# Gain rows by a broadcasting DMA instead of GpSimd, and other start addresses for token and weight tiles

## The chip, the cores and the metric

The kernel runs on one core of a Trainium2 chip. Its time is the device time of one execution in microseconds; lower is better. The core has five engines with instruction streams of their own: TensorE (PE in the profile, its weight loads as PEld), VectorE (DVE), ScalarE (ACT), GpSimd (POOL) and SyncE (SP), which here only issues transfers. Engines wait for each other by semaphores.

## What is computed

One decoder layer on 512 tokens of width 1024, float32: a SwiGLU block, a mixer that joins differential attention and an SSD scan, and a second SwiGLU block, each between two RMS norms with a gain row of 1024 values.

```python
def rms_norm(x, g):
    xf = x.astype(jnp.float32)
    y = xf * lax.rsqrt(jnp.mean(xf * xf, axis=-1, keepdims=True) + EPS)
    return (y * g.astype(jnp.float32)).astype(x.dtype)

def swiglu(h, w_gate, w_up, w_down):
    return (jax.nn.silu(h @ w_gate) * (h @ w_up)) @ w_down

def hybrid_layer(x, ...):
    h = rms_norm(x, ffn1_pre_g)
    x = x + 0.5 * rms_norm(swiglu(h, ffn1_w_gate, ffn1_w_up, ffn1_w_down), ffn1_post_g)
    h = rms_norm(x, mix_pre_g)
    proj = h @ w_in
    ...
    attn = diff_attention(q, k, v, lam, attn_subln_g, lambda_init)
    ssm = ssd_mixer(z, xbc, dt, conv_w, conv_b, dt_bias, a_log, d_skip, ssm_norm_g)
    mixed = jnp.concatenate([attn, ssm], axis=-1) @ w_out
    x = x + rms_norm(mixed, mix_post_g)
    h = rms_norm(x, ffn2_pre_g)
    x = x + 0.5 * rms_norm(swiglu(h, ffn2_w_gate, ffn2_w_up, ffn2_w_down), ffn2_post_g)
    return x
```

Seven gain rows are used: ffn1_pre, ffn1_post, mix_pre, mix_post, ffn2_pre (fetched twice, at the end of the mixer and at the start of the second block) and ffn2_post. Tokens lie on the 128 partitions where a norm is applied, so every partition needs the whole row.

## The kernel before

Three stages follow one another, `f1` (first SwiGLU), `mix` and `f2` (second SwiGLU). The 512 tokens are four tiles t = 0 to 3 of 128. A float32 operand is split into a high and a low part, and a product is three TensorE products (high x high, high x low, low x high): L219 to L221 are those of `mm3`, L396 the first lead product in another order, L450 the down projection, L327 the products of gate and up. These last go by a seven-product scheme over halves of the tokens and columns: VectorE and ScalarE make sums of weight halves (L286 to L309) and of token halves (L248 to L270), and 3360 products of 256 columns at L327 use them. Most weights come as 0.5 or 1 MB loads into `raw`, ScalarE casts the high part (L201, L291), VectorE subtracts the low part (L202, L292), and both stand in `w` in the SwiGLU stages and in `whi`/`wlo` in the mixer. `hb` holds the normalised, transposed tokens, `S` their sums, `hid` the hidden values, `ac` the accumulators.

A stage opens by normalising: the square and its sum on ScalarE (`sumsq`, L169), the reciprocal root on GpSimd (`rstd`, L162 a tensor_scalar, L163 a power with the constant `mhalf`), the scaling by root and gain on VectorE (L178), eight transposes per tile on TensorE (L183), the split into `hb` on ScalarE and VectorE (L187). In `f1` tiles 0 and 1 come first and the lead products follow; in `f2` tiles 0 and 1 are done as the mixer ends, and tiles 2 and 3 after the lead products of the first half of the tokens.

The gain of such a norm comes from `bcast` (L150 to L156): SyncE loads the row of 4 KB into one partition of a tile, and GpSimd's partition_broadcast (L155) writes it to all 128 partitions of a second tile. The 49 mixer parameters (`prm`, L140) go the same way. GpSimd also makes the 128x1024 products of the SSD steps (L808, tiles `kb` from `ah` and `al`), which L820 sums on TensorE (`decay`), sums of token halves (L248), masks, and it issues the stores of x. In the SSD steps TensorE goes by turns over attention (L748 transposes, L753 values), the decay products (L814, L820) and, as filler, projection products (L217 to L221); the gains `mix_post_g` and `ffn2_pre_g` are fetched there.

Within each engine the order is a list that a scheduler writes when the kernel is built; an instruction waits for its operands and for its buffer, and what stands behind it on its engine waits too. Tiles are placed one behind the other in the buffer in the order in which their tags first appear.

Of the kernel before, what the change touches and what calls it, by code (L numbers as in the profile page):

```python
# [11 lines left out]
F32 = mybir.dt.float32  # L12
# [5 lines left out]
P = 128  # L18
D = 1024
# [10 lines left out]
class Layer:  # L30
# [14 lines left out]
    @contextmanager  # L45
    def in_stage(s, name):

        with s.tc.tile_pool(name=name, bufs=1, reuse_waits="tile") as pool:
            s.stage, s.ffn_stage = pool, name != "mix"
            yield  # L50

    def blk(s, shape, dt=F32):
# [41 lines left out]
    def consts(s):  # L94
        nc = s.nc
        s.ident = s.t([P, P], F32, "ident")
        make_identity(nc, s.ident)
        s.mhalf = s.t([P, 32], F32, "mhalf")[:, :8]
        nc.gpsimd.memset(s.mhalf, -0.5)

    def mixer_consts(s, conv_w, conv_b, dt_bias, a_log, d_skip, subln, norm_g, lq1, lk1, lq2, lk2):
        nc = s.nc
        s.ones = s.t([P, P], F32, "ones")
        nc.gpsimd.memset(s.ones, 1.0)
        s.u1 = s.t([P, P], F32, "u1")
        nc.gpsimd.affine_select(s.u1, s.ones, pattern=[[-1, P]], base=-1, channel_multiplier=1,
                                compare_op=ALU.is_ge, fill=0.0)
        s.u2 = s.t([P, P], F32, "u2")
        nc.gpsimd.affine_select(s.u2, s.ones, pattern=[[1, P]], base=0, channel_multiplier=-1,
                                compare_op=ALU.is_ge, fill=0.0)  # L110

        rows = s.m((P, P))
        nr = 61 + 8
        nc.sync.dma_start(rows[0:48, :], conv_w.rearrange("k (t p) -> (k t) p", p=P))
        nc.sync.dma_start(rows[48:60, :], conv_b.rearrange("o (t p) -> (o t) p", p=P))
        nc.sync.dma_start(rows[60:61, 0:64], subln)
        nc.sync.dma_start(rows[60:61, 64:128], subln)
        nc.sync.dma_start(rows[61:69, :], norm_g.rearrange("o (t p) -> (o t) p", p=P))
        ps = s.pb()
        nc.tensor.transpose(ps[:, :nr], rows[:nr, :], s.ident[:nr, :nr])  # L120
        s.cols = s.t([P, nr], F32, "cols")
        nc.vector.tensor_scalar_mul(s.cols, ps[:, :nr], 0.5)
        nc.vector.tensor_scalar_mul(s.cols[:, 60:61], ps[:, 60:61], 1.0 - LAMBDA_INIT)

        row = s.m((1, 48 + 128))
        nc.sync.dma_start(row[:, 0:16], dt_bias)
        nc.sync.dma_start(row[:, 16:32], a_log)
        nc.sync.dma_start(row[:, 32:48], d_skip)
        for i, l in enumerate((lq1, lq2, lk1, lk2)):
            nc.sync.dma_start(row[:, 48 + 32 * i:80 + 32 * i], l)  # L130
        lam = s.t([1, 4], F32, "lam")
        nc.vector.tensor_mul(row[:, 48:112], row[:, 48:112], row[:, 112:176])
        nc.vector.tensor_reduce(lam[:, 0:2], row[:, 48:112].rearrange("p (a b) -> p a b", a=2),
                                axis=AX.X, op=ALU.add)
        nc.scalar.activation(lam[:, 0:2], lam[:, 0:2], AF.Exp)
        nc.scalar.activation(row[:, 16:32], row[:, 16:32], AF.Exp)
        nc.vector.tensor_scalar(row[:, 48:49], lam[:, 1:2], lam[:, 0:1], -LAMBDA_INIT,
                                op0=ALU.subtract, op1=ALU.add)
        s.prm = s.t([P, 49], F32, "prm")
        nc.gpsimd.partition_broadcast(s.prm, row[:, 0:49])  # L140
        s.nlam = s.prm[:, 48:49]

        s.qscale = s.t([P, 4], F32, "qscale")
        s.nslope = s.t([P, 48], F32, "nslope")[:, :16]
        for h in range(8):
            lo = (h % 2) * 64
            nc.gpsimd.memset(s.qscale[lo:lo + 64, h // 2:h // 2 + 1], 32.0 ** -0.5 * 2.0 ** (h + 1))
            nc.gpsimd.memset(s.nslope[:, 2 * h:2 * h + 2], -2.0 ** -(h + 1))

    def bcast(s, ap):  # L150
        nc = s.nc
        row = s.k4([1, D])
        nc.sync.dma_start(row, ap)
        t = s.k4([P, D])
        nc.gpsimd.partition_broadcast(t, row)  # L155
        return t  # L156


# [79 lines left out]
    def sums_of_h(s, h):  # L238

        nc, v = s.nc, s.nc.vector  # L240
        tmp = lambda: s.t([P, 4, 256], F32, "hid", 6, s.stage)
        a1 = []
        S1, S2, S3, S4 = (None,) * 4

        def first():
            for b in range(2):
                f = tmp()
                nc.gpsimd.tensor_tensor(f, h[b][0][:, :, :256].bitcast(F32), h[b][1][:, :, :256].bitcast(F32), op=ALU.add)  # L248
                a1.append(f)

        st = {}

        def more(t):
            ts = slice((t - 2) * P, (t - 1) * P)

            def f(p21, p22):
                if t == 2:
                    for n in range(1, 5):
                        st[n] = tmp()
                S1, S2, S3, S4 = (st[n][:, :, ts] for n in range(1, 5))  # L260
                a11, a12 = (a[:, :, ts] for a in a1)
                v.tensor_copy(S3, p21)
                v.tensor_sub(S1, p22, S3)
                v.tensor_sub(S3, a11, S3)
                v.scalar_tensor_tensor(S2, a11, -1.0, S1, op0=ALU.mult, op1=ALU.subtract)
                v.scalar_tensor_tensor(S4, a12, -1.0, S2, op0=ALU.mult, op1=ALU.subtract)
            return f

        def part(hi, lo, x):
            nc.scalar.copy(hi, x)  # L270
            v.tensor_sub(lo, x, hi)
            return hi, lo

        def end():
            A = {n: part(*(s.t([P, 4, 256], F32R, "S", 6, s.stage) for _ in range(2)), st[n]) for n in (3, 2, 4)}

            A[1] = part(*(h[0][i][:, :, 256:] for i in range(2)), st[1])
            return A

        return first, more, end  # L280
# [29 lines left out]

    def gate_up(s, A, wg, wu, i):

# [4 lines left out]
        def product(ps, a, b, first):  # L317
# [3 lines left out]
            for m in range(2):  # L321
                cs = slice(256 * m, 256 * m + 256)
                (ah, al), (wh, wl) = A[a], W[m][b]
                for k in range(4):
# [49 lines left out]
    def ffn(s, h, wg, wu, wd, gain, finish, prepare, fetch=(), late=()):  # L374
# [26 lines left out]
        for half in range(2):  # L401
            for i, (j, w) in enumerate(lead):
# [9 lines left out]
                product(banks[i], lw[i], slice(256 * half, 256 * half + 256), i == 0, ins if half == 0 else None)  # L412
        A = end()
        for b in range(2):
            for half in range(2):
                A.setdefault((11, 12)[b] + 10 * half, tuple(x[:, :, 256 * half:256 * half + 256] for x in h[b]))
        for pi, (i0, i1) in enumerate(parts):
# [721 lines left out]
```

## Time and profile before

| | us |
|---|---|
| median of 3 runs | 1156.06 (1155.16 to 1157.9) |
| the profiled execution | 1153.56 |
| its span | 1151.9 |
| PE busy in it | 1057.1 |
| DVE busy | 785.5 |
| ACT busy | 505.7 |
| POOL busy | 107.6 |

The span is the time from the first to the last record of the profiled execution. TensorE records are pipelined: the duration of one product (0.28 us for 256 columns) reaches beyond the start of the next, so the pace is read from start to start. A row of the timeline tells when an instruction started, how long it took and, in brackets, how long its engine had been idle and which engine ended that; "issue" there means that the profile shows nothing that it waited for. PEclk is the granted TensorE clock, 1.00 the upper of its two levels.

### The profile page before, as it was taken

To read this page: it belongs to the slowest core of one execution; us is meant where nothing else is said; L and a number is where in the kernel's file an instruction comes from. 1 tells how busy PE (TensorE), PEld (TensorE's weight loads), DVE (VectorE), ACT (ScalarE), POOL (GpSimd) and SP (SyncE) were. 2 spreads that over 40 slices of the span, in tenths; PEclk is the share of its full clock that TensorE was granted. 3 is DMA by queue.
4 is the path that set the end of the run, shared out by engine and by line. 5 is a ranking of instruction groups with operands and counts; after the bars stand their busy time and mean duration, and the time that the engine had idled before them with its cause. 6 is when DMAs were issued, how large, how long until landed. Compare 5 with 4: busy or idle time off the path is not lost. (4 is left out here: it accounts for less than half of the span.)

```text
span 1151.9 us, 16496 instructions
## 1 busy us (share of the span) xinstructions
PE 1057.1 (92%) x6569; PEld 943.2 (82%) x6569; DVE 785.5 (68%) x1189; ACT 505.7 (44%) x861; POOL 107.6 (9%) x132
## 2 busy tenths in 40 slices
PE   1999999999999789999996999967999999999997
PEld 1989898998898667888875777857898989988985
DVE  1977686775775733686885987675776867747745
ACT  2555343542453433465652455433653534524532
POOL 1300000000000310000013441031000000000001
PEclk9999999999999889999998999978999999999999
DMA  2523242242223254643321103054232422422232
GB/s 91 201 74 113 71 147 74 79 142 74 83 83 112 77 163 139 162 127 104 92 74 37 46 29 110 1 189 140 74 110 74 147 74 76 144 74 74 86 117 91
DMA packets 94821, 114.44 MB, mean 99 GB/s; under 512 B 5069, under 2 KB 74769, under 8 KB 94744
## 3 DMA queue, kind: packets, MB, share of 16 engines
q1 hardware_dynamic: 93592, 109.20, 30.4%
q0 software_dynamic: 1152, 4.19, 0.9%
q8 instruction: 51, 0.84, 0.3%
q14 instruction: 26, 0.21, 0.1%
HBM read 100.79 MB, written 6.29 MB: 93 GB/s over the span
## 5 line engine op out<-in xcount | busy, mean ns | idle before, releaser
L327 PE MATMUL pa<-hb,w 128*128 128x256 f32 x960 | 128.5, 284 | 5.7 <-DVE at L341 5.0
L327 PE MATMUL pa<-S,w 128*128 128x256 f32 x960 | 126.8, 283 | 4.3 <-ACT cv L357 4.3
L327 PE MATMUL pt<-hb,w 128*128 128x256 f32 x960 | 129.3, 283 | 0.6 <-DVE w L292 0.6
L327 PEld LDWEIGHTS pa<-hb,w 128*128 128x128 f32 x960 | 122.4, 192 | 8.8 <-DVE at L341 5.8
L327 PEld LDWEIGHTS pa<-S,w 128*128 128x128 f32 x960 | 120.7, 192 | 6.1 <-ACT cv L357 5.1
L327 PEld LDWEIGHTS pt<-hb,w 128*128 128x128 f32 x960 | 122.0, 192 | 1.6 <-DVE w L292 0.8
L292 DVE TENSOR_TENSOR w<-raw,w 128x1024 fp32r<-128x1024 f32 x80 | 97.6, 1221 | 30.9 <-PE pa L327 12.7
L202 DVE TENSOR_TENSOR w<-raw,w 128x1024 fp32r<-128x1024 f32 x52 | 72.0, 1395 | 58.2 <-PE pa L327 25.4
L291 ACT CAST w<-raw 128x1024 fp32r<-128x1024 f32 x80 | 83.9, 1049 | 57.9 <-PE pa L327 43.9
L450 PE MATMUL pb<-w,hid 128*128 128x512 f32 x384 | 96.8, 393 | 1.2 <-ACT hid L370 1.1
L201 ACT CAST w<-raw 128x1024 fp32r<-128x1024 f32 x52 | 54.0, 1048 | 95.9 <-PE pa L327 48.2
L450 PEld LDWEIGHTS pb<-w,hid 128*128 128x128 f32 x384 | 70.2, 189 | 14.5 <-ACT hid L370 1.6
L202 DVE TENSOR_TENSOR wlo<-raw,whi 128x1024 fp32r<-128x1024 f32 x44 | 53.3, 1221 | 36.3 <-ACT whi L201 36.0
L327 PE MATMUL pt<-S,w 128*128 128x256 f32 x480 | 64.0, 284 | 3.3 <-ACT S L270 2.5
L298 DVE TENSOR_TENSOR T<-raw 128x1024 f32<-128x1024 f32 x40 | 48.9, 1221 | 24.2 <-DMA raw<-in_ffn_w_up_dram 12.7
L155 POOL PARTITION_BROADCAST w<-w x5 | 6.7, 1342 | 620.1 <-DMA w<-in_ffn_post_g_dram 301.9
L450 PE MATMUL pa<-w,hid 128*128 128x512 f32 x192 | 64.5, 395 | 0.0
L220 PE MATMUL pa<-hb,whi 128*128 128x512 f32 x160 | 64.4, 402 | 0.0
L327 PEld LDWEIGHTS pt<-S,w 128*128 128x128 f32 x480 | 60.3, 191 | 4.7 <-ACT S L270 2.9
L221 PE MATMUL pa<-hb,wlo 128*128 128x512 f32 x160 | 64.1, 401 | 0.0
L201 ACT CAST whi<-raw 128x1024 fp32r<-128x1024 f32 x44 | 45.6, 1049 | 42.0 <-PE pa L220 32.8
L291 ACT CAST w<-T 128x1024 fp32r<-128x1024 f32 x40 | 42.1, 1052 | 44.4 <-PE po L450 22.6
(285 smaller groups left out, 2203.8 us busy)
## 6 DMA issues: line engine op xcount, KB each, us to landing
raw<-in_ffn_w_gate_dram SPq DMA_DIRECT2D x20, 1024.0 KB
raw<-in_ffn_w_up_dram SPq DMA_DIRECT2D x20, 1024.0 KB
raw<-in_ffn_w_down_dram SPq DMA_DIRECT2D x16, 1024.0 KB
raw<-in_w_in_dram SPq DMA_DIRECT2D x32, 512.0 KB
raw<-in_ffn_w_down_dram SPq DMA_DIRECT2D x12, 512.0 KB
blk<-kc SPq DMA_DIRECT2D x96, 64.0 KB
raw<-in_w_out_dram SPq DMA_DIRECT2D x12, 512.0 KB
x_d<-ac POOLq DMA_DIRECT2D x8, 512.0 KB, 4.9
```

The costliest lines, as they stand in the source:

```text
L155: nc.gpsimd.partition_broadcast(t, row)
L201: s.nc.scalar.copy(hi, raw)
L202: s.nc.vector.tensor_sub(lo, raw, hi)
L220: mm(ps, a[0], b[1], start=False, stop=False)
L221: return mm(ps, a[1], b[0], start=False, stop=last).ins
L291: nc.scalar.copy(hi, x)
L292: v.tensor_sub(lo, x, hi)
L298: v.tensor_add(T13.rearrange("p (h k) f -> p h k f", h=2), r[:, 0:4, :].rearrange("p k (h f) -> p h k f", h=2), odd.rearrange("p (h k) f - ...
L327: i = mm(ps[:, cs], x[:, k, :], y[:, k, :], start=first and head is None, stop=k == 3 and x is wl, skip_group_check=True)
L450: nc.tensor.matmul(pd[c], a[:, ts], w[:, c * S:(c + 1) * S], start=st, stop=sp)
```

## The change

1. `bcast` loads the row straight into all 128 partitions: one DMA whose source repeats the 4 KB row 128 times, 512 KB written. GpSimd's broadcast and the one-partition tile are gone.
2. `prm` is made by TensorE, a product of a row of ones with the 49 values into a PSUM bank, and a VectorE copy.
3. `mhalf` grows from 32 to 40 columns, a tile `place` of 64 bytes a partition is allotted at the head of the two SwiGLU stages, and another, `place_S`, ahead of `S`. Nothing is ever written to them: they move the start addresses of all that follows. As built, every large tile of the kernel before starts at a multiple of 128 bytes. After the change `hb`, `S`, `T` and `ac` start 32 bytes past such a multiple, `w`, `hid` and `raw` of the two SwiGLU stages 96 past, and all tiles of the mixer 32 past.

```diff
--- before.py
+++ after.py
@@ -47,6 +47,8 @@
 
         with s.tc.tile_pool(name=name, bufs=1, reuse_waits="tile") as pool:
             s.stage, s.ffn_stage = pool, name != "mix"
+            if s.ffn_stage:
+                s.t([P, 16], F32, "place", 1, pool)
             yield
 
     def blk(s, shape, dt=F32):
@@ -95,7 +97,7 @@
         nc = s.nc
         s.ident = s.t([P, P], F32, "ident")
         make_identity(nc, s.ident)
-        s.mhalf = s.t([P, 32], F32, "mhalf")[:, :8]
+        s.mhalf = s.t([P, 40], F32, "mhalf")[:, :8]
         nc.gpsimd.memset(s.mhalf, -0.5)
 
     def mixer_consts(s, conv_w, conv_b, dt_bias, a_log, d_skip, subln, norm_g, lq1, lk1, lq2, lk2):
@@ -137,7 +139,9 @@
         nc.vector.tensor_scalar(row[:, 48:49], lam[:, 1:2], lam[:, 0:1], -LAMBDA_INIT,
                                 op0=ALU.subtract, op1=ALU.add)
         s.prm = s.t([P, 49], F32, "prm")
-        nc.gpsimd.partition_broadcast(s.prm, row[:, 0:49])
+        ps = s.pb()
+        nc.tensor.matmul(ps[:, 0:49], s.ones[0:1, :], row[:, 0:49], start=True, stop=True)
+        nc.vector.tensor_copy(s.prm, ps[:, 0:49])
         s.nlam = s.prm[:, 48:49]
 
         s.qscale = s.t([P, 4], F32, "qscale")
@@ -149,10 +153,8 @@
 
     def bcast(s, ap):
         nc = s.nc
-        row = s.k4([1, D])
-        nc.sync.dma_start(row, ap)
         t = s.k4([P, D])
-        nc.gpsimd.partition_broadcast(t, row)
+        nc.sync.dma_start(t, ap.broadcast_to([P, D]))
         return t
 
 
@@ -272,6 +274,7 @@
             return hi, lo
 
         def end():
+            s.t([P, 16], F32, "place_S", 1, s.stage)
             A = {n: part(*(s.t([P, 4, 256], F32R, "S", 6, s.stage) for _ in range(2)), st[n]) for n in (3, 2, 4)}
 
             A[1] = part(*(h[0][i][:, :, 256:] for i in range(2)), st[1])
```

Lines from L155 on stand two or three lines further down in the changed kernel (L162 is L164 there, L183 is L185, L219 to L221 are L221 to L223, L327 is L330, L808 is L811, L820 is L823).

The scheduler gives another order at three places. SyncE's list at the start of `f1`, before (w_75 and w_76 are x's tiles 0 and 1, w_80 the gain):

```order
L1062 DMA w_75<-in_x_dram 128x1024
L153 DMA w_80<-in_ffn_pre_g_dram 1x1024
L210 DMA raw_137<-in_ffn_w_gate_dram 128x8x128
L210 DMA raw_168<-in_ffn_w_up_dram 128x8x128
L210 DMA raw_201<-in_ffn_w_gate_dram 128x8x128
L1062 DMA w_76<-in_x_dram 128x1024
L210 DMA raw_232<-in_ffn_w_up_dram 128x8x128
```

and now:

```order
L1065 DMA w_76<-in_x_dram 128x1024
L157 DMA w_81<-in_ffn_pre_g_dram 128x1024
L1065 DMA w_77<-in_x_dram 128x1024
L212 DMA raw_136<-in_ffn_w_gate_dram 128x8x128
L212 DMA raw_167<-in_ffn_w_up_dram 128x8x128
L212 DMA raw_200<-in_ffn_w_gate_dram 128x8x128
L212 DMA raw_231<-in_ffn_w_up_dram 128x8x128
```

The gain has become a full tile, and x's second tile has moved from behind three weight loads to right behind the gain.

GpSimd's list where the SSD steps begin, before; a bare "ISA" at a line is a change of its library, the ISA with ka tiles the broadcast:

```order
L808 TENSOR_TENSOR kb_5630<-u_545_3757,ah_4230 128x1024
L155 ISA
L155 ISA ka_6676<-ka_6674 128x1024
L808 ISA
L808 TENSOR_TENSOR kb_5632<-u_545_3757,al_4231 128x1024
L155 ISA
L155 ISA ka_6680<-ka_6678 128x1024
L808 ISA
L808 TENSOR_TENSOR kb_5648<-u_545_3757,ah_4230 128x1024
L808 TENSOR_TENSOR kb_5650<-u_545_3757,al_4231 128x1024
```

and now:

```order
L811 TENSOR_TENSOR kb_5628<-u_544_3753,ah_4228 128x1024
L811 TENSOR_TENSOR kb_5630<-u_544_3753,al_4229 128x1024
L811 TENSOR_TENSOR kb_5646<-u_544_3753,ah_4228 128x1024
L811 TENSOR_TENSOR kb_5648<-u_544_3753,al_4229 128x1024
L811 TENSOR_TENSOR kb_5764<-u_544_3753,ah_4228 128x1024
```

Six of the ten rows are gone, and the `kb` products of the first steps stand in a row. The same holds at every other broadcast; GpSimd's list has 129 rows where it had 151, and the only bare ISA left is the one at the masks at the very start.

TensorE's list at the start of `f2`, before (pa is the last lead product of the first half but one, po the last, pt and pb the transposes of tiles 2 and 3):

```order
L221 MATMUL pa_7011<-hb_6767,w_7008 128x256
L219 MATMUL po_7042<-hb_6765,w_7038 128x256
L183 MATMUL pt_7055<-ident_63,w_7053 128x128 x4
L183 MATMUL pt_7062<-ident_63,w_7053 128x128 x4
L220 MATMUL po_7042<-hb_6766,w_7038 128x256
L221 MATMUL po_7042<-hb_6765,w_7039 128x256
```

and now:

```order
L221 MATMUL po_7035<-hb_6759,w_7031 128x256
L222 MATMUL po_7035<-hb_6760,w_7031 128x256
L223 MATMUL po_7035<-hb_6759,w_7032 128x256
L221 MATMUL po_7035<-hb_6761,w_7031 128x256
L222 MATMUL po_7035<-hb_6762,w_7031 128x256
L185 MATMUL pt_7048<-ident_63,w_7046 128x128 x4
L185 MATMUL pt_7055<-ident_63,w_7046 128x128 x4
L223 MATMUL po_7035<-hb_6761,w_7032 128x256
L185 MATMUL pb_7079<-ident_63,w_7077 128x128 x4
```

The transposes of tile 2 stood behind the first product of po; they now stand behind its first 14, and those of tile 3 one product later.

## Rows read from the trace of the kernel before

**Rows 1.** The page, part 1: engine, busy us (share), xinstructions.

```profile
PE 1057.1 (92%) x6569; PEld 943.2 (82%) x6569; DVE 785.5 (68%) x1189; ACT 505.7 (44%) x861; POOL 107.6 (9%) x132
```

**Rows 2.** Waits of PE: waiting <- awaited: us in total, times, longest.

```profile
PE pt L183 <- DVE w L178: 30.1, 3, 22.0
PE pb L820 <- POOL kb L808: 12.2, 2, 10.1
```

**Rows 3.** Line 155: ns min/median/max, first to last start us.

```profile
L155 POOLq MODIFY_POOL_CONFIG  x12: 1/11/15, 1.6 to 792.8; - x12
L155 POOL PARTITION_BROADCAST w<-w x5: 1302/1302/1499, 12.1 to 1093.2; - x5
```

**Rows 4.** Timeline of POOL, start: us, duration, instruction, [idle <-releaser].

```profile
12.09 1.30 POOL L155 PARTITION_BROADCAST w<-w  x1 [10.47 <-issue]
20.33 0.18 POOL L162 TENSOR_SCALAR r<-ss 128x1 f32<-128x1 f32 x1 [6.94 <-issue]
```

**Rows 5.** Windows: PE, PEld, DVE, ACT, POOL busy, PEclk, DMA, GB/s.

```profile
4.00:10.00 6.00, 0.00 (x0) 0.00 (x0) 0.00 (x0) 1.15 (x2) 0.00 (x0) 1.00 1.06 335
10.00:20.00 10.00, 0.00 (x0) 0.00 (x0) 0.00 (x0) 0.00 (x0) 1.30 (x1) 1.00 0.01 3
```

**Rows 6.** Timeline of ACT and PE, the start.

```profile
4.53 1.06 ACT L169 ACTIVATE w<-w 128x1024 f32<-128x1024 f32 x1 [2.46 <-DMA w<-in_x_dram]
24.52 1.06 ACT L169 ACTIVATE w<-w 128x1024 f32<-128x1024 f32 x1
29.22 2.08 PE L396 MATMUL pa<-hb,w 128*128 128x256 f32 x8
```

**Rows 7.** Timeline of POOL, the start of the SSD steps.

```profile
590.44 1.84 POOL L155 PARTITION_BROADCAST ka<-ka  x1 [6.39 <-PE pt L748]
600.05 1.89 POOL L808 TENSOR_TENSOR kb<-u,al 128x1024 fp32r<-128x1024 f32 x1 [7.77 <-PE pt L748]
607.87 1.56 POOL L155 PARTITION_BROADCAST ka<-ka  x1 [5.93 <-ACT cv L594]
616.55 1.89 POOL L808 TENSOR_TENSOR kb<-u,ah 128x1024 fp32r<-128x1024 f32 x1 [7.12 <-issue]
```

**Rows 8.** Timeline of PE, the start of the SSD steps.

```profile
618.49 1.22 PE L820 MATMUL pb<-kb,u1r 128*128 128x512 f32 x2 [10.11 <-POOL kb L808]
619.51 0.63 PE L217 MATMUL pa<-hb,whi 128*128 128x512 f32 x1
...
621.64 0.54 PE L221 MATMUL pa<-hb,wlo 128*128 128x512 f32 x1
...
622.48 0.40 PE L217 MATMUL pa<-hb,whi 128*128 128x512 f32 x1
...
625.92 0.39 PE L217 MATMUL pa<-hb,whi 128*128 128x512 f32 x1
```

**Rows 9.** Timeline of POOL and ACT, the start of f2.

```profile
778.61 1.31 POOL L155 PARTITION_BROADCAST w<-w  x1 [5.94 <-issue]
789.68 0.18 POOL L162 TENSOR_SCALAR r<-ss 128x1 f32<-128x1 f32 x1 [9.77 <-issue]
779.55 1.04 ACT L169 ACTIVATE w<-ac 128x1024 f32<-128x1024 f32 x1
```

**Rows 10.** Timeline of PE, the start of f2.

```profile
783.84 0.28 PE L219 MATMUL po<-hb,w 128*128 128x256 f32 x1
792.01 1.94 PE L183 MATMUL pt<-ident,w 128*128 128x128 f32 x8 [7.89 <-DVE w L178]
...
794.18 0.41 PE L219 MATMUL po<-hb,w 128*128 128x256 f32 x1
794.39 0.41 PE L220 MATMUL po<-hb,w 128*128 128x256 f32 x1
```

**Rows 11.** Windows, columns as in Rows 5: products in f2.

```profile
980.00:1000.00 20.00, 20.00 (x167) 19.96 (x166) 14.88 (x22) 12.56 (x22) 0.00 (x0) 1.00 0.40 142
```

**Rows 12.** The page, part 5: a group of line 327.

```profile
L327 PE MATMUL pa<-hb,w 128*128 128x256 f32 x960 | 128.5, 284 | 5.7 <-DVE at L341 5.0
```

## The prediction

> **What bounds the kernel now.** I read the engine totals first. TensorE is busy 1057.1 of the 1151.9 us span, 92%, and VectorE 68% [rows 1]; so the time is TensorE's own work plus the stretches in which it stands still, and the second thing to read is what it stood still for. Two of its waits are larger than any other: the transposes of L183 waited 30.1 us in three pieces, the longest 22.0, for VectorE's scaled rows, and L820 waited 12.2 us in two pieces for a GpSimd product [rows 2]. Both lead to GpSimd, which is busy only 9% [rows 1]. So I read its instructions around those waits, and what it did before each. Line 155, the partition broadcast, costs 1.30 us itself and comes with pool-configuration commands, 12 of them on that line [rows 3]. What is long is the silence around it: 10.47 us before the first broadcast and 6.94 us before the tiny operation that follows it, which belongs to the other library [rows 4]. The same pair stands around every broadcast: 6.39 and 7.77, 5.93 and 7.12 us in the SSD steps [rows 7], 5.94 and 9.77 us at the start of f2 [rows 9]. Five of the eight end by "issue", that is, on nothing the profile shows; the other three have the same length, so I read all eight as the switch of libraries.
>
> There are eight broadcasts, seven of gains and one of parameters. Four of them, two ahead of the first FFN's end, one ahead of the second's and that of the parameters, hold up nothing that TensorE waits for. The other four stand at three places, which I take in order.
>
> **Part 1: the start.** x's first tile is there at 4.53 us, and the square of the second stands at 24.52, queued on ScalarE behind casts that need the first scaled tile; the first product follows at 29.22, 4.70 us after that square [rows 6]. All loads are in at about 10 us: 335 GB/s from 4 to 10, 3 GB/s after [rows 5]. After the change the first scaled tile waits for x, the gain and a reciprocal root, no library. The gain is now 512 KB instead of 4 KB; on SyncE's queue it stands behind x's first tile and the second tile right behind it, ahead of the weights. At 335 GB/s it takes 1.6 us, so the gain is in at about 6.1 and the second tile at 7.7; the square of that tile then runs 4.70 us before the first product: 12.4, and I take 13 for the fixed part of two transfers. Weights (512 KB each, behind) land from 9.3 on and are cast in about 1 us, in time. Gain: 29.2 - 13 = 16, of which I take 15.5. Its ends are 14 (128 reads of the same 4 KB at half the rate, 1.6 us more) and 16.5.
>
> **Part 2: the start of the SSD steps.** The first wait there is 12.2 - 10.1 = 2.1 us, the second 10.1 [rows 2]. In the new order the four kb products stand in a row with no switch between, so the second is no longer held for 7.77 us behind a broadcast, nor the third for 7.12 [rows 7]. SyncE's loads there ask for one tile of the ka buffers instead of two each, so nothing new is waited for. During the long wait the clock fell: products of 512 columns come every 426 ns afterwards (five steps from 619.51 to 621.64) and every 229 ns once it is back (15 steps from 622.48 to 625.92) [rows 8]; these are the levels of 1.2 and 2.4 GHz. Six products and a pair at L820 run at the lower level: 7 x 0.2 = 1.4 us, and about 0.4 us for the pair. Sum 2.1 + 10.1 + 1.8 = 14. Ends 11 (a wait of one product's 1.89 us remains, and part of the clock) and 15.
>
> **Part 3: the start of f2.** TensorE stops after 783.84 and goes on at 792.01 [rows 10], because the reciprocal root started at 789.68 though the squares it reads were finished by 780.6 (the second starts at 779.55 and takes 1.04) [rows 9]. Without the switch the root is there about 1 us after the square, VectorE's scaling 1.3 us later, at 783. The new order also puts 13 products ahead of the transposes, another 1.6 us of cover. So the stop goes: 792.01 - 783.96 = 8.05. The clock adds ten products at 213 ns (794.18 to 794.39) [rows 10] instead of 120 (20.00 us hold 167) [rows 11], 0.9, and transposes at half rate, 0.7. Sum 9.6, ends 7 (the first weight sums on VectorE become the late thing) and 10.
>
> **What it adds.** Seven broadcasts now move 512 KB each, 3.5 MB in all. On SyncE's queue each stands where its row stood, so the loads behind it shift by 1.6 us. Only the start and f2 have full queues; elsewhere loads run ahead. The parameter broadcast becomes one product of 49 columns and a VectorE copy; the nearest row, eight transposes in 1.94 us at half rate [rows 10], puts it at 0.25 us on TensorE, and it is ready before TensorE reaches it. I take 1 us for all this; ends 0 and 4.
>
> Sum of the broadcast part: 15.5 + 14 + 9.6 - 1 = 38. From the profiled run's own 1153.56 us (the span and 1.7 around it) this gives 1115.5; the median of the runs is 2.5 us above that run, so about 1118 without any effect of the placement.
>
> **The placement.** In before every large tile starts at a multiple of 128 bytes. Afterwards, in L327 and the lead products, the moving tile (hb, S) starts 32 past and the stationary one (w) 96 past; in L450 both are at 96, in the mixer both at 32. So L327 alone gets two operands that differ, by 64. Its pair of weight load and product takes 20.00/167 = 120 ns [rows 11]. At the lower clock the same pair takes 213 [rows 10], and half of that is 107: a pair at full clock carries 13 ns that are not columns. The pair of 512 columns carries nearly as much: 229 against 426/2 = 213, 16 ns [rows 8]. An extra that is one size for both widths, and gone at the lower clock, is not a matter of the columns but of something that happens once a pair. Each pair loads 128 columns of weights while the product before streams. If the two streams get into each other's way in the buffer, then equal offsets are the likeliest to meet, and the new offset changes that for L327: four groups of 960, 960, 960 and 480, of which one stands in [rows 12], 3360 pairs. No row has another offset, so I bound it: all of the 13 ns gone, 44 us; none, 0; as much again, 44 us lost. I take half of it, 6.7 ns: 22 us. VectorE is busy 14.88 of 20 us in that stretch [rows 11], which would be 79% of the shorter one, so its late moments grow; I give back a quarter and keep 17 us. The sum is 38 + 17 = 55, so 1156 - 55 = **1101**.
>
> One page bears on this term. The Trainium skill (TensorE: Matmul & The Clock Gate, Wait — 56ns, not 53.3ns?) gives a product at full clock 2.5 ns above its columns; the rows show 13, so they do not agree with it in this layout. By the page an undisturbed L327 pair would take about 109 ns and the time would be 1082 to 1091, an estimate; that is the lower part of B below.
>
> **Rivals.**
> *A, the placement is neutral:* the 13 ns is a fixed price of a pair with 4-byte operands. For it: it is nearly the same at both widths, in the mixer and in the FFN [rows 8, 11]. Then 1111 to 1122, centre 1118. Chance 0.34.
> *B, the forecast:* L327 runs faster, between 2 and 12 ns a pair, 1075 to 1111. Chance 0.47.
> *C, the broadcast gains shrink:* either the reads of one row are slow and the loads behind them late, or offsets of 32 and 96 cost the transfers. Transfers are at their limit only in short stretches (the start, 335 GB/s [rows 5]); half again of those 6 us is 3 us. Or the pair gets up to 5 ns dearer, 17 us in L327. 1122 to 1150. Chance 0.12. The Trainium skill (DMA: Bandwidth & Descriptors, How a descriptor splits into AXI transactions) says that a descriptor that doesn't start on 256 bytes needs one transaction more, which speaks against the offsets; no row here shows such a tile. By it the start would lose about those 3 us.
> *D, slower than before:* the pairs get dearer in all stages, since 32 and 96 are off the 128-byte grid everywhere. It decides once the pairs cost 38 us more over TensorE's 6569 products [rows 1], 5.8 ns each, near half of today's 13 again. For it: that the 13 are there at all with every tile on the grid. Against it: only the FFN's products get operands that differ; in the mixer and in L450 both move alike. At 9 ns it would be 1118 + 59 = 1177. Chance 0.06.
> That the change doesn't do what it says, the switches staying, is excluded: GpSimd's new order holds no broadcast and no switch but the first. Within 0.2%, which is about what can be told from no change here, is left with 0.01.
>
> **The numbers.** The range of 8 in 10 takes A whole and B but for its lowest few us: 1078 to 1122. Faster by over 0.2%: A, B, C, 0.93; slower 0.06.
>
> **What would show it.** The first L396 at about 13 us instead of 29.2; GpSimd with no silence ended by "issue" beyond the start; no wait over 2 us of L823 for GpSimd, none of L185 for VectorE at f2's start. The placement is read from one number: how many L327 products stand in 20 us of undisturbed work; 167 is A, 177 is B, under 160 is C or D. I would be wrong by far if the first product came after 16 us, if L327's waits for VectorE (now a few us) took up what the pair gives, or if a pair went over 126 ns.

## The result and the profile after

The changed kernel takes 1109.22 us (median of 4 runs, 1106.99 to 1111.67) against 1155.61 us of the kernel before on the same chip: a ratio of 0.9602, with a 95% interval of 0.9569 to 0.9634. It is 46.4 us faster. The forecast was 1101, in a range of 1078 to 1122. Of the five runs of one kernel below, that with the rows alone, two were disturbed, the profiled one among them (1315.83 us at a mean clock of 0.75, and 5854.25 us), so its time is the median of the other three and no row of its trace is read.

The profiled execution has a span of 1107.1 us. Part 1 of its page (the columns as in [rows 1]):

```profile
PE 1045.1 (94%) x6571; PEld 931.3 (84%) x6571; DVE 784.4 (71%) x1190; ACT 507.6 (46%) x861; POOL 95.4 (9%) x124
```

TensorE's busy time fell by 12.0 us and its share rose from 92 to 94%; most of the 44.8 us that the span lost were stops. The three largest waits of TensorE now (columns as in [rows 2]):

```profile
PE pt L185 <- DVE w L180: 11.8, 2, 7.7
PE pa L399 <- ACT w L203: 5.5, 1, 5.5
PE pa L330 <- DVE at L344: 5.1, 4, 1.3
```

The wait of L820 (L823 here) for GpSimd, 12.2 us in [rows 2], has no row any more. What is left of the 30.1 us at the transposes is the 7.7 us until x, gain and root are there at the start, and one stop of 4.1 us at the end of the first block, which the profile before put to another releaser (L132).

The start. GpSimd's first roots, the squares of x's first two tiles on ScalarE, and TensorE (timelines, columns as in [rows 4]):

```profile
6.05 0.19 POOL L164 TENSOR_SCALAR r<-ss 128x1 f32<-128x1 f32 x1 [4.68 <-ACT w L171]
9.15 0.19 POOL L164 TENSOR_SCALAR r<-ss 128x1 f32<-128x1 f32 x1 [2.27 <-ACT w L171]
```

```profile
4.82 1.06 ACT L171 ACTIVATE w<-w 128x1024 f32<-128x1024 f32 x1 [2.75 <-DMA w<-in_x_dram]
7.92 1.06 ACT L171 ACTIVATE w<-w 128x1024 f32<-128x1024 f32 x1 [1.95 <-DMA w<-in_x_dram]
```

```profile
7.72 1.97 PE L185 MATMUL pt<-ident,w 128*128 128x128 f32 x8 [7.72 <-DVE w L180]
10.98 1.97 PE L185 MATMUL pb<-ident,w 128*128 128x128 f32 x8 [1.29 <-DVE w L180]
12.77 1.44 PE L399 MATMUL pa<-hb,w 128*128 128x256 f32 x5
```

The root starts at 6.05 us where it started at 20.33 [rows 4], with no silence that ends by "issue", and the first lead product at 12.77 where it was 29.22 [rows 6]. The square of the second tile waits for that tile's load until 7.92. In the window from 4 to 10 us (columns as in [rows 5]) the transfers run at nearly the rate of before:

```profile
4.00:10.00 6.00, 1.97 (x8) 1.57 (x8) 1.84 (x3) 3.05 (x6) 1.51 (x5) 1.00 1.00 323
```

The start of the SSD steps, GpSimd, then TensorE:

```profile
562.61 1.92 POOL L811 TENSOR_TENSOR kb<-u,ah 128x1024 fp32r<-128x1024 f32 x1 [8.23 <-PE pt L751]
570.99 2.36 POOL L811 TENSOR_TENSOR kb<-u,al 128x1024 fp32r<-128x1024 f32 x1 [6.47 <-PE pt L751]
577.91 1.90 POOL L811 TENSOR_TENSOR kb<-u,ah 128x1024 fp32r<-128x1024 f32 x1 [4.56 <-DVE wlo L204]
580.52 1.90 POOL L811 TENSOR_TENSOR kb<-u,al 128x1024 fp32r<-128x1024 f32 x1 [0.71 <-issue]
```

```profile
575.49 0.64 PE L823 MATMUL pb<-kb,u1r 128*128 128x512 f32 x2
...
577.14 0.62 PE L823 MATMUL pb<-kb,u1r 128*128 128x512 f32 x2
```

Between the two `kb` products for the first decay step (562.61 and 570.99) there is no broadcast any more, which in [rows 7] stood there with its two silences; the second ends at 573.35, ahead of the L823 at 577.14 that reads it, and the next two follow at 577.91 and 580.52. TensorE has no stop here. But 6.47 us of silence, ended by a transpose of L751, stand between the first two without any broadcast, so the 6.39 and 7.77 us of [rows 7], which transposes ended too, are not shown to have been switches alone.

The start of f2, GpSimd, then VectorE's scaling of tile 2, then TensorE:

```profile
746.20 0.19 POOL L164 TENSOR_SCALAR r<-ss 128x1 f32<-128x1 f32 x1 [7.22 <-ACT w L171]
746.47 0.57 POOL L165 TENSOR_TENSOR r<-r,mhalf 128x1 f32<-128x1 f32 x1
747.24 1.17 POOL L164 TENSOR_SCALAR r<-ss 128x1 f32<-128x1 f32 x1 [0.20 <-ACT w L171]
```

```profile
747.08 1.28 DVE L180 SCALAR_TENSOR_TENSOR w<-ac,r,w 128x1024 f32<-128x1024 f32 x1 [0.76 <-POOL r L165]
```

```profile
749.70 0.28 PE L221 MATMUL po<-hb,w 128*128 128x256 f32 x1
...
751.29 1.03 PE L185 MATMUL pt<-ident,w 128*128 128x128 f32 x8
752.28 1.04 PE L185 MATMUL pb<-ident,w 128*128 128x128 f32 x8
```

The root of tile 2 starts at 746.20, 0.1 us after ScalarE's sum of the square, where [rows 9] had 9.77 us of silence, and the transposes of tiles 2 and 3 run at full clock, 1.0 us each instead of 1.94 [rows 10], without a wait. The scaled tile 2 is there at 748.36, ahead of the first product of `po` at 749.70 behind which the transposes stood in the old order; so it is the earlier root that takes this stop away, and the 13 products put ahead were not needed for it.

Gate and up products in a window of 18 us inside one uninterrupted unit of 168 of them (3360 are 20 such units), in f1 and in f2, after and then before (columns: PE busy (x count), PEld busy (x), PEclk, DMA share, GB/s):

```profile
205.40:223.40 18.00, 18.00 (x157) 18.00 (x156) 1.00 0.35 112
931.30:949.30 18.00, 18.00 (x158) 18.00 (x156) 1.00 0.33 108
```

```profile
223.30:241.30 18.00, 18.00 (x152) 18.00 (x152) 1.00 0.39 131
974.00:992.00 18.00, 18.00 (x152) 18.00 (x151) 1.00 0.31 102
```

157 and 158 products stand in 18 us instead of 152 (one or two at the edges are counted that lie partly outside). Over all gate and up products of 256 columns, the lead products among them, the mean from start to start (values over 130 ns, stops and lower clock, left out) is 116.5 ns where the moving tile is `hb` and 117.9 where it is `S`, against 119.8 before for both; over those of L330 alone it is 116.9 with `hb`. The means further down are taken in the first way.

Between the starts of the same instructions in the two traces the 44.8 us divide so (us):

| stretch | before | after | change |
|---|---|---|---|
| to the first lead product (L396) | 29.22 | 12.77 | -16.45 |
| from there to the first L327 | 16.49 | 17.81 | +1.32 |
| L327 of f1, first to last | 322.09 | 317.20 | -4.89 |
| to the first mixer product | 41.67 | 41.60 | -0.07 |
| to the first L820 | 185.57 | 186.11 | +0.54 |
| to the 16th L820 | 57.56 | 43.26 | -14.30 |
| to f2's first lead product | 115.59 | 115.74 | +0.15 |
| to the transposes of tile 2 | 23.81 | 16.79 | -7.02 |
| to the first L327 of f2 | 8.67 | 5.54 | -3.13 |
| L327 of f2, first to last | 318.69 | 317.74 | -0.95 |
| to the last product | 23.61 | 23.65 | +0.04 |

The three stops give 16.45 + 14.30 + 10.15 = 40.9, 2.0 go back in small pieces, and the gate and up products give 5.8.

### The profile page after: what moved, and what is told of

The parts are those of the page before. It is cut to its first block, busy times and chain, and to the rows that moved or that the text cites. A ratio compares the mean times of both kernels' runs of the same rounds, so it can differ in the third digit from the quotient of the medians.

```text
span 1107.1 us, 16447 instructions
## 1 busy us (share of the span) xinstructions
PE 1045.1 (94%) x6571; PEld 931.3 (84%) x6571; DVE 784.4 (71%) x1190; ACT 507.6 (46%) x861; POOL 95.4 (9%) x124
## 4 chain that ended last, share of the span: by engine, by line
PE 53%; DVE 5%; SPq 2%; DMA 2%; issue 2%; ACT 2%; POOL 1%; DVEq 0%; POOLq 0%; ACTq 0%
PE pa L330 10%; PE pt L330 7%; PE pa L222 6%; PE pa L223 6%; PE pa L219 4%; PE pb L453 4%; SPq L581 2%; PE pa L221 2%; PE pa L453 2%; PE po L453 2%; DMA raw<-in_ffn_w_gate_dram 1%; PE po L843 1%; PE po L756 1%; PE pb L724 1%; DVE w L295 1%
## 5 line engine op out<-in xcount | busy, mean ns | idle before, releaser
L330 PE MATMUL pa<-hb,w 128*128 128x256 f32 x960 | 126.1, 282 | 6.7 <-DVE at L344 5.1
L330 PE MATMUL pa<-S,w 128*128 128x256 f32 x960 | 125.4, 280 | 4.4 <-ACT cv L360 4.4
L330 PEld LDWEIGHTS pa<-hb,w 128*128 128x128 f32 x960 | 120.0, 190 | 10.1 <-DVE at L344 5.9
L330 PE MATMUL pt<-hb,w 128*128 128x256 f32 x960 | 126.6, 280 | 0.2 <-DVE w L295 0.2
L330 PEld LDWEIGHTS pa<-S,w 128*128 128x128 f32 x960 | 118.9, 188 | 6.2 <-ACT cv L360 5.2
L330 PEld LDWEIGHTS pt<-hb,w 128*128 128x128 f32 x960 | 118.9, 189 | 1.0 <-DVE w L295 0.4
L164 POOL TENSOR_SCALAR r<-ss 128x1 f32<-128x1 f32 x32 | 14.5, 453 | 785.8 <-DVE ss L502 722.6
L330 PE MATMUL pt<-S,w 128*128 128x256 f32 x480 | 63.4, 281 | 3.7 <-ACT S L272 3.0
L330 PEld LDWEIGHTS pt<-S,w 128*128 128x128 f32 x480 | 59.6, 188 | 5.3 <-ACT S L272 3.4
L223 PE MATMUL pa<-hb,wlo 128*128 128x512 f32 x160 | 63.7, 398 | 0.0
```

The costliest lines, as they stand in the source:

```text
L223: return mm(ps, a[1], b[0], start=False, stop=last).ins
L330: i = mm(ps[:, cs], x[:, k, :], y[:, k, :], start=first and head is None, stop=k == 3 and x is wl, skip_group_check=True)
```

## Experiments

**The two parts apart.** First the rows and the parameters without the placement:

```diff
-                s.t([P, 16], F32, "place", 1, pool)
-        s.mhalf = s.t([P, 40], F32, "mhalf")[:, :8]
+        s.mhalf = s.t([P, 32], F32, "mhalf")[:, :8]
-            s.t([P, 16], F32, "place_S", 1, s.stage)
```

> Rows by DMA and the parameters by TensorE, no placement (every large tile at a multiple of 128 bytes, as before). Theory: the two parts add up. The changed kernel's trace puts 16.5 us at the first product, 14.3 in the SSD steps and 10.2 at the start of f2 against 2.5 given back in f2's first unit, and 8.3 us on the pace of the gate and up products (4.9 in f1, 3.4 in f2's units after the first). Without placement that pace goes back from about 117 to 120 ns and the time is 1156 - 38 = 1118, ratio to before 0.966 to 0.969. Rival: the faster pace comes from the broadcasts' going (GpSimd's silence, other transfers), not from the addresses; then 117 ns and about 1109, ratio 0.960.

Measured: 1114.80 us (three runs, 1113.27 to 1117.85), ratio 0.9662 (0.9636 to 0.9688), which is 39.0 us of the 1154.5 of before. Then the placement alone, on the kernel before:

```diff
+                s.t([P, 16], F32, "place", 1, pool)
-        s.mhalf = s.t([P, 32], F32, "mhalf")[:, :8]
+        s.mhalf = s.t([P, 40], F32, "mhalf")[:, :8]
+            s.t([P, 16], F32, "place_S", 1, s.stage)
```

> Placement alone on the kernel before; GpSimd still broadcasts. Theory: gate and up products at 117 ns, 40 products of 512 columns as before, and 1156 - 8 = 1148 (ratio 0.992 to 0.995); the three stops stay as they were (first product at 29, 10 us at L820, 8 us at f2's transposes). Rival: the addresses are worth nothing by themselves; 120 ns and a ratio of 0.998 to 1.002.

Measured: 1147.58 us, ratio 0.9940 (0.9925 to 0.9955), 6.9 us. The gate and up products in 18 us of a unit of f1 and of f2 (columns as above):

```profile
219.10:237.10 18.00, 18.00 (x157) 18.00 (x156) 1.00 0.43 142
969.90:987.90 18.00, 18.00 (x157) 18.00 (x156) 1.00 0.34 115
```

The counts are those of the changed kernel, with GpSimd's broadcasts still there: the first lead product is at 28.35 us, where it was 29.22. So the two parts add up within their intervals, 39.0 + 6.9 = 45.9 against 46.4, and the pace is a matter of the addresses. The rival, that the pace came with the broadcasts' going, falls on both runs.

**Are the silences the switch of GpSimd's library?** The changed kernel with one small broadcast put back that nothing waits for as data:

```diff
         nc.gpsimd.memset(s.mhalf, -0.5)
+        nc.gpsimd.partition_broadcast(full[:, 8:16], s.mhalf[0:1, :])
```

> The changed kernel with one GpSimd partition broadcast of 8 unused values at its very start; nothing reads them but the order on GpSimd. All data come as in the changed kernel. Theory, that the silences are switches of GpSimd's library: about 10 us before the broadcast and 7 after it come back, the first reciprocal root starts at 18 to 20 us instead of 6 and the first product at 25 to 29 instead of 12.8; the time is 12 to 16 us longer than the changed kernel's. Rival, that the broadcast waited for its row or for a buffer: it runs at 2 to 3 us, and the first product stays at about 13.

Measured: 1122.41 us in one run. GpSimd at the start, and TensorE's first lead product (L401 here):

```profile
11.04 0.28 POOL L103 PARTITION_BROADCAST mhalf<-mhalf  x1 [9.42 <-issue]
18.53 0.18 POOL L166 TENSOR_SCALAR r<-ss 128x1 f32<-128x1 f32 x1 [7.21 <-issue]
```

```profile
25.20 4.00 PE L401 MATMUL pa<-hb,w 128*128 128x256 f32 x20
```

The operand of this broadcast is a constant written at 0.93 us, and still it starts at 11.04 after 9.42 us of silence; the root, whose square was there before 6 us, starts at 18.53 after 7.21. The first lead product slips from 12.77 to 25.20, 12.4 us, and the time by 13.2. That is 12.4 of the 16.45 us that the start gave; the other 4.0 (29.22 - 25.20) stay, and go with the new order of the transfers, by which x's second tile is squared at 7.92 in this run too. A wait for the row or for a buffer is excluded here: the two silences come with the operation, whatever it reads. The Trainium skill (GPSIMD Engine Reference, Instruction dispatch) says that the first call of freshly loaded code pays about 6 us more; the silences before a broadcast or behind one are 5.9 to 10.5 us in the kernel before and 7.2 and 9.4 here, so the page's figure is about the lowest of them.

**Does a switch cost wherever it stands?** The changed kernel with GpSimd's broadcast back at four of the eight places, those ahead of the end of the two blocks and the parameters:

```diff
+                    by_pool = key in ("post1", "post2")
-                    nx[key] = s.bcast(row)
+                    nx[key] = s.bcast(row, by_pool)
...
-        nc.tensor.matmul(ps[:, 0:49], s.ones[0:1, :], row[:, 0:49], start=True, stop=True)
-        nc.vector.tensor_copy(s.prm, ps[:, 0:49])
+        nc.gpsimd.partition_broadcast(s.prm, row[:, 0:49])
```

> The changed kernel with GpSimd's broadcast back at four of the eight places: both gains fetched before the end of the first block, the one before the end of the second, and the 49 parameters; DMA at the start, in the SSD steps and at the start of f2. Theory, that these four lie beside other work: within 2 us of the changed kernel's 1109 (ratio to before 0.958 to 0.963). Rival, that each switch costs wherever it stands (some 8 us each): 1125 and more.

Measured: 1109.65 us, ratio 0.9582 (0.9556 to 0.9609), not to be told from the changed kernel. Two of its broadcasts on GpSimd's timeline:

```profile
323.18 1.30 POOL L158 PARTITION_BROADCAST w<-w  x1 [298.81 <-DVE at L346]
325.08 1.67 POOL L158 PARTITION_BROADCAST w<-w  x1 [0.60 <-DVE cv L356]
```

The first stands behind 298.81 us without any work for GpSimd, and the second, right behind it, starts after 0.60 us: between two broadcasts in a row there is no such silence. All the gain of the rows is at the four broadcasts behind which something was queued that TensorE waits for.

**Which offset counts?** Four kernels with the token tiles (`hb`, `S`) at one place and the weight tiles `w` a chosen distance further, another distance in f1 than in f2. The distance is the start address of the stationary tile (the one that is loaded as weights) less that of the moving tile (the one that streams through), modulo 256 bytes:

```diff
-        s.mhalf = s.t([P, 40], F32, "mhalf")[:, :8]
+        s.mhalf = s.t([P, 8], F32, "mhalf")[:, :8]
-        s.nslope = s.t([P, 48], F32, "nslope")[:, :16]
+        s.nslope = s.t([P, 16], F32, "nslope")[:, :16]
             if s.ffn_stage:
-                s.t([P, 16], F32, "place", 1, pool)
+                s.place = {"f1": (32, 0), "f2": (0, 32)}[name]
+                if s.place[0]:
+                    s.t([P, s.place[0]], F32, "place", 1, pool)
...
-            s.t([P, 16], F32, "place_S", 1, s.stage)
+            if s.place[1]:
+                s.t([P, s.place[1]], F32, "place_S", 1, s.stage)
```

The numbers in the third change are those of the first of the four, 0 and 128.

> The changed kernel with other addresses: token tiles 32 past a multiple of 128; in f1 the weight tiles at the same offset (difference 0), in f2 128 bytes further (difference 128 of 256). Theory that the difference between weight and token tiles decides: 120 ns a product in f1, as before, though all tiles are off the 128-byte grid; in f2 120 as well if 128 bytes repeat, another value if not. Rival, that leaving the grid decides: 117 ns in f1.

Measured: 1115.84 us in one run. Windows of 18 us in f1 (0) and f2 (128):

```profile
206.50:224.50 18.00, 18.00 (x153) 18.00 (x152) 1.00 0.38 126
936.80:954.80 18.00, 18.00 (x154) 18.00 (x153) 1.00 0.34 110
```

The mean from start to start is 119.8 ns in f1, as in the kernel before, with every tile 32 bytes off the grid: leaving the grid alone does nothing. In f2 it is 119.1.

> The changed kernel with other addresses: in f1 the weight tiles start 64 bytes past both hb and S (of 256), in f2 64 bytes before both. In the changed kernel the difference is +64 for hb (mean 116.5 ns a product, 29% at 115 or less) and -64 for S (117.8 ns, 1%). Theory, that the difference of the addresses alone decides, with its sign: 116.5 in f1 and 117.8 in f2, for hb and S alike. Rival, that hb and S differ by their shape (rows of 2 KB against 1 KB): hb 116.5 and S 117.8 in both stages.

Measured: 1107.54 us in one run. Windows in f1 (+64) and f2 (-64):

```profile
203.50:221.50 18.00, 18.00 (x161) 18.00 (x160) 1.00 0.44 149
928.90:946.90 18.00, 18.00 (x155) 18.00 (x155) 1.00 0.36 108
```

Means: +64 gives 115.3 for `S` and 115.7 for `hb`, -64 gives 117.8 for both. So the shape of the tile is not the cause of the difference between `hb` and `S` in the changed kernel; it has `S` on the other side of `w`.

> The same with a difference of +32 bytes in f1 and -32 in f2. Theory, that a collision between the two streams depends on their distance: values between that of 0 (119.8) and of 64 (116.5 to 117.8), about 118. Rival, that only being off the same 64-byte half counts: 119.8 as with 0.

Measured: 1112.68 us in one run; +32 gives 118.3, -32 gives 116.9, for both tiles. The rival is wrong; the theory is right for +32 alone, since -32 is quicker than -64 and not slower.

> The same with +96 bytes in f1 and -96 in f2. By the theory of distance 96 lies between 64 (116.5 to 117.8) and 128 (119.1): about 118; below 116 it would be the better place, worth up to 3360 x 1 ns and more.

Measured: 1116.28 us in one run. Windows in f1 (+96) and f2 (-96):

```profile
206.30:224.30 18.00, 18.00 (x156) 18.00 (x155) 1.00 0.35 108
936.60:954.60 18.00, 18.00 (x152) 18.00 (x152) 1.00 0.30 97
```

Means: +96 gives 118.1, as expected, -96 119.9, as slow as 0. The map of eight distances, mean ns of a pair of 256 columns:

| distance | 0 | +32 | +64 | +96 | 128 | -96 | -64 | -32 |
|---|---|---|---|---|---|---|---|---|
| ns | 119.8 | 118.3 | 115.5 | 118.1 | 119.1 | 119.9 | 117.8 | 116.9 |

None is dearer than 0 by more than 0.1 ns, and equal addresses are not alone at the top. Distances other than 0, +64 and -64 stand on one run each, and the mean at +64 alone goes from 113.7 to 116.7 in the kernels of this document, so the order of close values is not shown.

**The same distance for 512 columns?** These kernels had shifted the mixer's weights by 128 against `hb`, and its products had risen from 229 to 232.5 ns. So all others were moved as well:

```diff
+        pads = {"hid": s.place[2]} if s.ffn_stage else {"whi": 48, "blk": 16}
+        if pool is not None and pool is s.stage and pads.get(tag) and tag not in s.moved:
+            s.moved.add(tag)
+            pool.tile([P, pads[tag]], F32, tag="place_" + tag, name=f"place_{tag}_{s.n}", bufs=1)
```

> The changed kernel with a difference of +64 bytes (of 256, weight tile past moving tile) for every gate and up product in both stages; in the mixer the high weights 64 past hb and blk 64 past the weights; in the down projection the hidden tiles 64 past the weights in f1 and 64 before them in f2. Theory, that the same distance counts for products of 512 columns: the down projection falls from 227.8 ns by 2 to 4 in f1 and by about 2 in f2, the mixer's products by 2 to 4 where the stationary tile is 64 past the moving one; gate and up at 115.5 in both stages. Sum 3360 x 1.5 + some 1500 x 3 = 10 us: about 1100. Rival, that a pair of 512 columns has its 16 ns from elsewhere: 227.8 stays in both stages and the time is about 1104.

Measured: 1106.57 us in one run. The gate and up products are at 114.2 to 114.7 ns; the down projection at 233.0 in f1 (+64) and 229.2 in f2 (-64) instead of 227.8, the mixer's products at 233 where the distance is +64. The theory that the widths go together is wrong, and so is its rival: the distance counts for 512 columns too, and there +64 is a bad one. So the best of each was joined, with the changed kernel beside it on the same chip:

```diff
-        pads = {"hid": s.place[2]} if s.ffn_stage else {"whi": 48, "blk": 16}
+        pads = {"hid": s.place[2]} if s.ffn_stage else {"whi": 32, "blk": 0}
-                s.place = {"f1": (48, 32, 16), "f2": (48, 0, 48)}[name]
+                s.place = {"f1": (48, 48, 0), "f2": (48, 48, 0)}[name]
```

> The changed kernel with +64 bytes (of 256) between weight and moving tile for all gate and up products, and difference 0 again for all products of 512 columns (mixer and down projection). The run before this one showed 114.5 ns a gate and up product at +64, and 233 ns at +64 for products of 512 columns against 227.8 to 229 at 0. Theory, that every group keeps the pace of its own distance wherever the others are: 114.5 to 115.5 ns and 227.8 ns, so 5 to 8 us (3360 products, 1.6 to 2.6 ns less than the changed kernel's 117.1 mean) under the changed kernel: 1101 to 1104. Rival, that the L330 pace depends on the neighbours' addresses or that the gain is given back at the stalls: within 3 us of the changed kernel.

> The changed kernel itself on the chip of the run above, to compare the two without the difference of chips: 1109, ratio to before 0.957 to 0.963.

Measured: 1106.15 us, ratio 0.9585 (0.9558 to 0.9612), beside 1108.95, 0.9606 (0.9582 to 0.9631), for the changed kernel. 2.8 us less, with intervals that overlap: a tendency, not a shown gain, and the rival's "within 3 us" rather than the theory's 1101 to 1104. Its windows in f1 and f2:

```profile
206.30:224.30 18.00, 18.00 (x155) 18.00 (x154) 1.00 0.43 143
930.20:948.20 18.00, 18.00 (x161) 18.00 (x160) 1.00 0.36 126
```

155 and 161 products: with the same addresses modulo 256 in both stages the pace is not the same. (The whole addresses are not the same: as built, the weights of most products lie in another of their buffers in f2 than in f1.) The means are 116.2 to 116.4 in f1 and 115.8 to 116.1 in f2, where 114.5 was expected; single pairs take either about 113 or about 118 ns, and the share of the quick ones changes (31 to 46% here, 70 to 83% in the run before). The two kinds come in long stretches: in this trace 3155 of 3179 successive pairs of L339 (the gate and up products there) are of the same kind as the one before, and of the two windows, which hold the same products of the two stages, one is slow (150 of 152 pairs of 117 to 119 ns), one quick (all of 113 or 114).

The last one moved only the products of 512 columns again:

```diff
-        pads = {"hid": s.place[2]} if s.ffn_stage else {"whi": 32, "blk": 0}
+        pads = {"hid": s.place[2]} if s.ffn_stage else {"whi": 40, "blk": 8}
-                s.place = {"f1": (48, 48, 0), "f2": (48, 48, 0)}[name]
+                s.place = {"f1": (48, 40, 8), "f2": (48, 8, 40)}[name]
```

> Only the products of 512 columns are moved against e10_mixed: hidden tiles 32 past the weights in f1 and 160 in f2 (of 256), mixer weights 32 past hb, blk 32 past the weights. So far 0 gave 227.8 to 229, 64 gave 233, 128 gave 232.5, 192 gave 229 to 230.6. Theory, that 0 is the best place for this width: 229 to 233 everywhere. Rival, that a better one lies between: below 227 at 32, 160 or 224.

Measured: 1108.02 us in one run. Windows of gate and up products, then a row of the down projection in the chain of waits (start us, us, what), and the same row of the changed kernel:

```profile
204.70:222.70 18.00, 18.00 (x161) 18.00 (x161) 1.00 0.46 149
931.70:949.70 18.00, 18.00 (x162) 18.00 (x161) 1.00 0.41 132
```

```profile
844.95 5.60 PE pb L462 x24
```

```profile
843.82 5.48 PE pb L453 x24
```

24 products of 512 columns take 5.60 us instead of 5.48, 233 against 228 ns, at 32 and 160 as at 64 and 128; 0 is the best of the seven distances that were run at this width. But the gate and up products, whose own distance did not change, went to 113.7 to 114.3 ns, 80 to 94% of them quick. What was lost on one width about came back on the other. In both kernels L339 starts slow behind products of 512 columns (42 of 42 times in the run before, 41 of 42 here), but a slow pair is followed by a quick one 16 times in 2069 there and 50 times in 252 here. What brings that change sooner was not settled; the two runs with most quick pairs are those with the down projection off distance 0.

## Why the prediction was right, and where not

The direction, the mechanism of the three stops and the range held; 46.4 us came where 55 were forecast. That the range held says little of the placement, since it takes in 1111 to 1122, where the placement does nothing. Rival B's lower end is 1078 by its own terms (12 ns on 3360 pairs from 1118), not 1075; nothing hangs on it.

- Part 1, the start: 15.5 forecast, 16.45 measured; the first lead product at 12.77 for "about 13". The gain's 512 KB cost what 335 GB/s says: x's second tile was squared at 7.92 for 7.7, 3.1 us after the first, for two transfers of 512 KB.
- Part 2, the SSD steps: 14 forecast, 14.30 measured. All four silences there were read as switches though the profile named other releasers for three. The small broadcast put back shows a switch at the start; of those in the SSD steps only the 7.12 us that end by "issue", ahead of the product for which TensorE stood 10.1 us, are of that kind by the profile, and 6.47 us ended by a transpose remain ahead of the second product. No run put a broadcast back here, so how much of the 14.30 us the switches alone are stays open.
- Part 3, the start of f2: 9.6 forecast, 10.15 measured, stop and clock together.
- What it adds: 1 us forecast; 1.3 us between the first lead product and the first L327, 0.5 us ahead of the first L820, 0.2 after. The rows alone gave 39.0 us for a forecast sum of 38.
- The placement: the mis-sized term. It was put at 6.7 ns a pair. The pair of L330 fell by 2.9 ns with `hb` and 1.95 with `S`, together 1920 x 2.9 + 1440 x 1.95 = 8.4 us, and 6.9 came out at the end in the run of the placement alone. That a quarter is given back is not shown: the two stretches of L330 fell by 5.8 us in the table above, but by 8.5 (5.1 in f1, 3.4 in f2) in the changed kernel's second profile. By the prediction's own sign 174 products stand in 20 us of f2, between the 167 of A and the 177 of B (columns as in [rows 5]):

```profile
935.00:955.00 20.00, 20.00 (x174) 20.00 (x173) 15.72 (x23) 11.70 (x17) 0.00 (x0) 1.00 0.36 117
```

The step that failed is "I take half of it": nothing in the trace carried it, and the reason beside it, that equal offsets are the likeliest to meet, does not hold, since -96 is as slow as 0 and for 512 columns 0 is the best place found.
- Rival A (neutral, 1111 to 1122) is refuted by the run of the placement alone, though the time of 1109 lies close to its edge. Rival C's dear transfers did not come: 323 GB/s at the start against 335 [rows 5]. 12 GB/s less over those 6 us are 0.2 us at most, and the window holds other work as well. By the Trainium skill (DMA: Bandwidth & Descriptors, How a descriptor splits into AXI transactions) a descriptor that doesn't start on 256 bytes fetches from the boundary below it; the page tells this of reads, and the loads at the start read from the same places as before, only the tiles that they write are moved. Rival D needed dearer pairs; the dearest that any distance gave was 119.9 against 119.8 at 256 columns and 5 ns more at 512, which the change does not touch.
- "VectorE's late moments grow" was right in kind. f2's first unit, where VectorE is busy 85% of the time (36.6 of 43.1 us), kept nothing of the pace. Windows over that unit, in the changed kernel, in its second profile (that of the run beside the joined kernel) and in the kernel before (columns as in [rows 5]):

```profile
756.83:802.27 45.44, 42.20 (x294) 38.92 (x293) 37.31 (x47) 23.84 (x34) 0.00 (x0) 0.96 0.27 86
```

```profile
756.21:799.33 43.12, 40.32 (x294) 37.50 (x293) 36.56 (x46) 23.64 (x34) 0.00 (x0) 1.00 0.26 84
```

```profile
800.68:843.63 42.95, 41.03 (x294) 38.43 (x293) 36.61 (x47) 23.96 (x34) 0.00 (x0) 1.00 0.24 81
```

45.44 and 43.12 us for the same kernel, the first with a mean clock of 0.96 in that stretch, against 42.95 before. So the gain of only 0.95 us that the table shows for f2 is low mostly by one execution's clock: in the second profile f2's L327 took 315.33 us, 3.4 less than before, and the first unit has no part in it.

## What to carry to other kernels

An engine that is 9% busy can still hold up the one that is 92% busy: read the silences on both sides of its odd instruction, and count only those behind which something is queued that the bound engine waits for; four of eight broadcasts made all of the 39 us. A broadcast from memory by DMA costs its bytes (1.6 us for 512 KB here) and no switch. Where the operands of a matmul start relative to each other is worth a scan by experiment, per width of the moving tile, and not by reasoning: at 256 columns it was worth up to 4 ns a pair, and the best place there cost 5 ns a pair at 512. One run per place is not enough where the same distance gave 113.7 to 116.7 ns in different kernels.

## What the runs showed of the hardware that was not expected

- The time of a pair of weight load and product at the upper clock depends on the distance between the stationary and the moving tile in the buffer: at 256 columns from 119.9 ns (-96) and 119.8 (0) to 115.5 (+64), with sign, and at 0 the same 119.8 with all tiles on the grid and 32 bytes off it; at 512 columns 227 to 230 at 0, and in every group of products 1.4 to 6 more at each other distance that was run. Why it does is open. The Trainium skill (TensorE: Matmul & The Clock Gate, Wait — 56ns, not 53.3ns?) has one fixed extra of 2.5 ns a product, which would be 109 at 256 columns, an estimate. No distance reached it in the mean.
- At +64 a pair takes either about 113 or about 118 ns, each kind in long stretches, and the share of the quick ones goes from 25 to 94% between kernels and stages. In the joined kernel it differs between two stages with the same addresses modulo 256. So the distance alone does not set the pace; what else does is left open.
- The two silences around a GpSimd broadcast come back with a broadcast of 8 constants (9.42 and 7.21 us); they do not depend on the size or the source of what is broadcast. A second broadcast right behind another has none (0.60 us).
